# FFN output products of a hybrid layer as seven block products in one sweep over all tokens

## The chip, the cores and the metric

One core of a Trainium2 chip runs the whole layer as one program. The metric is the device time of one execution in microseconds (us), as the median of several runs. Beside the runs one execution was profiled; all rows below come from its trace.

## What is computed

The layer is one block of a decoder with 1024 tokens and a width of 1024. The parts that matter here are the two feed-forward networks (FFN), which have the same form:

```
def _swiglu(x, w_in, w_out):
    h = x @ w_in                                  # 1024x1024 @ 1024x5632
    gate, up = jnp.split(h, 2, axis=-1)           # 2816 columns each
    return (jax.nn.silu(gate) * up) @ w_out       # 1024x2816 @ 2816x1024

x = _layer_norm(ALPHA * x + 0.5 * _swiglu(x, ffn1_w_in, ffn1_w_out), ln1_g, ln1_b)
proj = x @ mix_w_in                               # z_a, z_u, z_v, two gates
...                                               # SSM branch, gMLP branch, merge, LN2
x = _layer_norm(ALPHA * x + 0.5 * _swiglu(x, ffn2_w_in, ffn2_w_out), ln3_g, ln3_b)
x = x + sigmoid(x @ ple_w_gate) * (p @ ple_w_proj)
```

All data is float32. Each operand of a product is cut into a high part and a low part (both float32r), and a product is the sum of three: high x high, high x low, low x high.

## The kernel before

**Engines.** TensorE executes in the order of the program text. ScalarE and VectorE get an order that a scheduler works out when the kernel is built, from its own estimate of times; a group at the start is an exception. Loads of weights go out on SP's queue, stores and loads of residual rows on POOL's. `split(hi, lo, src)` (L72) makes the parts of an operand: a ScalarE copy with a cast (L74) and a VectorE subtraction (L75).

**Jobs.** All weight loads of the kernel form one list (`add_job`, `make_jobs`, L204). Raw tiles of 128x1024 (512 KB) come through three buffers (`RAWBUFS`), split tiles `hi` and `lo` through five of each (`WBUFS`). `take(key, AHEAD)` asks for a job and for the three after it. Work that is to run between later matmuls is put off with `defer(us, key, fn)`: `tick()` in the product loops runs what is due by a running sum of TensorE time, and `need(key)` runs it at the latest.

**Gate and up products (`hidden`, L506).** There are 22 steps f. Each makes the gate and the up block of 128 columns for all tokens, as seven block products (Strassen in Winograd's form) of 12 matmuls of 128x128 by 128x512. The sums of weights for a step are made by `pair_steps` (L282) on VectorE. Of the three PSUM banks of a step, `b1` is copied out and added to further: the product that follows the next one waits for the copy. The results stay in `es` (tiles `e0` to `e3`; `e0` and `e1` have two buffers, the others one) and are stored to DRAM, `g_d[f]`, by two DMAs (L556). Two pairs of FFN 2 are split during FFN 1 (`PRE_AT`), stored, and loaded again.

**Output products (`out_phase`, L563).** Tokens are eight tiles (tt) of 128 rows, done in three sweeps (`SWEEPS`): tiles 0 to 2, 3 to 5, 6 and 7. A sweep holds two PSUM banks of 128x512 for each tile and goes over all 22 chunks f. For each f it needs the 128x1024 rows of `w_out`, split (kept for the last five f between sweeps, else loaded again), and the activations of its tiles, 128x384 or 128x256, loaded by `load_g` and split (L74 `gh`, L75 `gl`). The first two chunks are split before the phase begins (`early`, tile `ge`). At a sweep's end VectorE adds the banks to the residual row tile y (L609), then `norm_tile` (L436) normalizes y, TensorE transposes it and `to_T` splits it into `xh` and `xl` (L75), and POOL multiplies and adds the norm's vectors for the residual (`keep`, L736 and L737). In the sweeps that are followed by another, this is put off by 6 to 18 us of TensorE time.

**What follows.** After FFN 1 `z_block` (L757) multiplies the new x by the weights of z_v, z_a and z_u, four token tiles at a time with four split units on the chip. `snake` (L478) goes through the four units forward and backward in turn; the turn is kept over the whole kernel. After FFN 2 the last stage (`ppg`, `ppp`) uses the same `snake`, two token tiles at a time.

## Time and profile before

| | us |
|---|---|
| median of 3 runs | 2128.04 (2123.31 to 2128.73) |
| the profiled execution | 2132.67 |
| its span, first to last instruction | 2130.9 |
| gate and up products of FFN 1, one step of 22 | 19.6 |
| output phase of FFN 1 (first output matmul to first of z_v) | 471.2 to 723.5 |
| output phase of FFN 2 (to the end of its matmuls) | 1754.8 to 2006.2 |

The profiled execution is 4.6 us above the median of the runs, and its span is 1.8 us short of its time. Busy time of TensorE counts matmuls that overlap in its pipeline, so that a mean duration near 400 ns in a row says nothing of the pace; the distance between two starts does.

### The profile page before, as it was taken

The numbers are of one execution on the slowest core, as the hardware profiler recorded it, in microseconds if no ns is written. First come the engines' busy times: TensorE is split into PE (matmuls) and PEld (weight loads), VectorE is DVE, ScalarE is ACT, GpSimd is POOL, SyncE is SP. The second block draws the span as 40 slices with busy tenths as digits, with TensorE's granted clock in tenths as the row PEclk, the third lists the DMA queues.
The fourth block names the chain that finished last, engine by engine and source line by source line (L and its number), as shares of the span: only waits on it lengthen the run. The fifth ranks groups of instructions, "written<-read, shape, count | busy, mean of one in ns | idle before, by whom it ended". The sixth has DMA issues, their size and how long they took to land.

```text
span 2130.9 us, 25814 instructions
## 1 busy us (share of the span) xinstructions
PE 2104.5 (99%) x9471; PEld 1718.0 (81%) x9471; DVE 1264.3 (59%) x2327; ACT 796.5 (37%) x1317; POOL 314.0 (15%) x367
## 2 busy tenths in 40 slices
...
GB/s 139 89 79 159 89 142 105 79 142 251 120 222 139 195 56 50 74 82 71 99 55 233 288 229 238 96 82 80 89 69 80 89 100 313 149 165 141 151 60 40
DMA packets 212413, 273.21 MB, mean 128 GB/s; under 512 B 18196, under 2 KB 159088, under 8 KB 212288
## 3 DMA queue, kind: packets, MB, share of 16 engines
...
## 4 chain that ended last, share of the span: by engine, by line
PE 84%; issue 6%; DVE 5%; DMA 2%; ACT 1%; POOL 1%; SPq 0%; POOLq 0%; DVEq 0%; ACTq 0%
PE p_f L502 36%; PE po_f L465 8%; PE po_f L463 8%; PE po_f L464 8%; PE ppg L464 1%; PE ppg L463 1%; PE ppg L465 1%; PE po_mo L463 1%; PE po_mo L464 1%; PE po_mo L465 1%; PE pgb L463 1%; PE pga L463 1%; PE pga L464 1%; PE pga L465 1%; PE pgb L464 1%
## 5 line engine op out<-in xcount | busy, mean ns | idle before, releaser
L75 DVE TENSOR_TENSOR wl<-wr,wh 128x1024 fp32r<-128x1024 f32 (+1 forms) x212 | 253.0, 1196 | 129.6 <-ACT wh L74 129.6
L74 ACT CAST wh<-wr 128x1024 fp32r<-128x1024 f32 (+1 forms) x212 | 203.4, 960 | 223.8 <-issue 43.0
L463 PE MATMUL po_f<-wh,gh 128*128 128x512 f32 x680 | 270.8, 398 | 0.0
L465 PE MATMUL po_f<-wh,gl 128*128 128x512 f32 x680 | 268.8, 395 | 0.0
L464 PE MATMUL po_f<-wl,gh 128*128 128x512 f32 x680 | 268.7, 395 | 0.0
L556 POOL DMA_DIRECT2D g_d<-e_f x88 | 47.9, 544 | 776.3 <-DVE e_f L553 742.3
L74 ACT CAST gh<-gr_f 128x384 fp32r<-128x384 f32 (+1 forms) x128 | 60.9, 476 | 245.8 <-PE po_f L464 206.5
L465 PEld LDWEIGHTS po_f<-wh,gl 128*128 128x128 f32 x680 | 127.6, 188 | 31.1
L464 PEld LDWEIGHTS po_f<-wl,gh 128*128 128x128 f32 x680 | 127.7, 188 | 29.9
L463 PEld LDWEIGHTS po_f<-wh,gh 128*128 128x128 f32 x680 | 127.7, 188 | 29.8
L75 DVE TENSOR_TENSOR gl<-gr_f,gh 128x384 fp32r<-128x384 f32 (+1 forms) x128 | 67.0, 527 | 114.7 <-ACT gh L74 114.1
L292 DVE TENSOR_TENSOR s<-wr 128x512 f32<-128x512 f32 x44 | 30.9, 703 | 165.4 <-DMA wr<-in_ffn_w_in_dram 165.4
L75 DVE TENSOR_TENSOR wlt<-s,wht 128x1024 fp32r<-128x1024 f32 x44 | 53.9, 1226 | 53.4 <-ACT wht L74 51.0
L74 ACT CAST whs<-s 128x1024 fp32r<-128x1024 f32 x44 | 46.1, 1049 | 80.7 <-PE p_f L502 71.9
L74 ACT CAST wht<-s 128x1024 fp32r<-128x1024 f32 x44 | 46.1, 1048 | 76.4 <-PE p_f L502 76.0
L502 PE MATMUL p_f<-T3l,wht 128*128 128x512 f32 (+3 forms) x184 | 72.2, 393 | 1.9 <-DVE T3l L75 1.9
L502 PE MATMUL p_f<-B11l,wha 128*128 128x512 f32 (+3 forms) x184 | 72.1, 392 | 1.5 <-DVE B11l L75 1.5
L502 PE MATMUL p_f<-T4h,wh 128*128 128x512 f32 (+3 forms) x184 | 72.1, 392 | 0.8 <-ACT e_f L546 0.8
L75 DVE TENSOR_TENSOR xl<-xf_x,xh 128x512 fp32r<-128x512 f32 x32 | 62.8, 1969 | 16.9 <-ACT xh L74 16.8
L502 PE MATMUL p_f<-T4l,wh 128*128 128x512 f32 (+3 forms) x184 | 72.1, 392 | 0.4 <-DVE T4l L75 0.4
L502 PE MATMUL p_f<-T3h,wht 128*128 128x512 f32 (+3 forms) x184 | 72.3, 393 | 0.0
L502 PE MATMUL p_f<-B11h,wha 128*128 128x512 f32 (+3 forms) x184 | 72.2, 392 | 0.0
...
## 6 DMA issues: line engine op xcount, KB each, us to landing
wr<-in_ffn_w_out_dram SPq DMA_DIRECT2D x112, 512.0 KB, 3.7
wr<-in_ffn_w_in_dram SPq DMA_DIRECT2D x88, 512.0 KB, 4.2
...
wr<-in_mix_w_in_dram SPq DMA_DIRECT2D x28, 512.0 KB, 3.8
x_d<-y POOLq DMA_DIRECT2D x16, 512.0 KB, 4.3
...
xs<-in_x_dram SPq DMA_DIRECT2D x8, 512.0 KB, 8.3
```

The source lines that it names most:

```text
L74: ACT.copy(out=hi, in_=src)
L75: DVE.tensor_sub(out=lo, in0=src, in1=hi.bitcast(F32))
L292: DVE.tensor_tensor(out=s1, in0=a21, in1=a22, op=ALU.add)
L463: PE.matmul(acc, lhsT=ah, rhs=bh, start=start, stop=False)
L464: PE.matmul(acc, lhsT=ah, rhs=bl, start=False, stop=False)
L465: PE.matmul(acc, lhsT=al, rhs=bh, start=False, stop=stop)
L502: PE.matmul(acc[:, cs], lhsT=p, rhs=q, start=start and k == 0 and i == 0, stop=stop and k == HK - 1 and i == 2, skip_group_check=True)
L556: nc.gpsimd.dma_start(out=g_d[f][:, h * HT:(h + 1) * HT], in_=es[h])
```

## The change

Both output phases become seven block products in the same Winograd form as the gate and up products. The 2x2 blocks are: tokens in two halves of 512 (four tiles each), hidden columns in pairs of chunks (even and odd f), and output columns in two halves of 512. A product goes over 11 chunk pairs, and its four PSUM banks (one for each token tile of a half) stay open over the next products: each is evicted after a product and then added to. So each product evicts 128x512 four times, 28 times in all, and the token tiles 0 to 3 are complete after the fifth product and the tiles 4 to 7 after the seventh (`OUT`, `out_strassen`).

Operands that are sums are made before. After each odd step `hidden` makes four sums of activations on VectorE (`total`) and stores seven blocks of 128x512 in place of two for each of two steps. A job `wsum` for each pair of chunks loads two row tiles of `w_out`, makes four differences in place on VectorE and stores both tiles to DRAM (`wt_d`). In the output phase each of the 77 units then loads 128x512 of weights and 128x512 of activations by two DMAs into one raw tile, which is split as a whole.

The rest follows from the order: all eight residual tiles of FFN 1 have buffers of their own; `norm_half` puts off the first half's tiles in steps of 11 us and the second half's in steps of 6.5 us; the second half of z_v is done tile by tile (five calls of `snake` where there were two); units of the stage after the phase are no longer asked for inside it; and the pre-made pairs and the vector transposes move.

```diff
-SWEEPS = ((0, 1, 2), (3, 4, 5), (6, 7))
 PSWEEPS = ((0, 4, 1), (5, 2, 6), (3, 7))
-PRE_AT = (9, 15)
-LN_US = 13.0
+OUT = (("S1", "T1", False, 1, 1, True, False), ("S4", "B22", True, 0, 1, True, False),
+       ("A12", "B21", False, 0, 0, True, False), ("A11", "B11", False, 0, 0, False, False),
+       ("S2", "T2", True, 0, 1, False, True), ("S3", "T3", True, 1, 1, False, False), ("A22", "T4", True, 1, 0, True, True))
+GX = ("A11", "A12", "A22", "S1", "S2", "S3", "S4")
+NP = NF // 2
+PRE_AT = (8, 14)
 LN2_US = 13.0, 10.0, 8.5
...
+    def ffn_jobs(nm, w_in, w_out, g_d):
+        rows = lambda f: w_out[f * P:(f + 1) * P, :]
         for f in range(NF):
             pair = lambda w, f: [[(0, 1024, cols(w, f * P, P))], [(0, 1024, cols(w, FF + f * P, P))]]
             if nm == "f1" and f in PRE_AT:
                 add_job(("pre", PRE_AT.index(f)), "pre", pair(w2i, PRE_AT.index(f)))
+            if f % 2:
+                add_job((nm, "ws", f // 2), "wsum", [[(0, 1024, rows(f - 1))], [(0, 1024, rows(f))]])
             add_job((nm, "h", f), "pair", [] if nm == "f2" and f < len(PRE_AT) else pair(w_in, f))
-        out_jobs(nm, w_out, NF, sweeps)
-
+        for p, (a, b, *_) in enumerate(OUT):
+            for i in range(NP):
+                y, x = {"T1": (0, 0), "T3": (0, 1), "T4": (1, 0), "T2": (1, 1)}.get(b, (int(b[1]) - 1, int(b[2:] or 0) - 1))
+                w = wt_d[nm][i][y] if b[0] == "T" else rows(2 * i + y)
+                add_unit((nm, "s", p, i), [(0, 512, w[:, x * 512:(x + 1) * 512]), (512, 512, g_d[i][a])])
+    g1_d, g2_d = ([{x: dram.tile([P, HT], F32, name=f"g_{nm}_{i}_{x}") for x in GX} for i in range(NP)] for nm in ("f1", "f2"))
+    wt_d = {nm: [[dram.tile([P, D], F32, name=f"wt_{nm}_{i}_{y}") for y in range(2)] for i in range(NP)] for nm in ("f1", "f2")}
...
+            elif kind == "wsum":
+                (b11, b12), (b21, b22) = ((r[:, :512], r[:, 512:]) for r in loaded[li:li + 2])
+                for o, x, y in ((b11, b12, b11), (b12, b22, b12), (b22, b22, b11), (b21, b21, b22)):
+                    DVE.tensor_tensor(out=o, in0=x, in1=y, op=ALU.subtract)
+                for y in range(2):
+                    nc.gpsimd.dma_start(out=wt_d[key[0]][key[2]][y], in_=loaded[li + y])
...
-    def norm_tile(y, tt, nm, transposed, keep, wait=0.0, ln_us=LN_US):
-
-
-        def first():
-            normalize(y, D, f"{nm}_{tt}")
-            defer(ln_us + wait / 2, ("x", tt), lambda: transposed((0,)))
+    def norm_tile(y, tt, nm, transposed, keep, t0, t1, wait=0.0):
         def rest():
             transposed((1,))
             keep()
         if wait:
-            defer(wait, ("x", tt), first)
+            defer(wait, ("n", tt), lambda: normalize(y, D, f"{nm}_{tt}"))
         else:
-            first()
-        defer(wait * 1.5 + ln_us + 1.9 + (4.0 if wait else 0.0), ("x", tt), rest)
+            normalize(y, D, f"{nm}_{tt}")
+        defer(t0, ("x", tt), lambda: transposed((0,)))
+        defer(t1, ("x", tt), rest)
+    def norm_half(y, tt, *a):
+        h, j = divmod(tt, 4)
+        if h:
+            norm_tile(y, tt, *a, 9.0 + 6.5 * j, 11.5 + 6.5 * j)
+        else:
+            norm_tile(y, tt, *a, 17.0 + 11.0 * j, 21.0 + 11.0 * j, 3.0 + 11.0 * j)
...
             if cs.stop == HT:
-                for h in range(2):
-                    nc.gpsimd.dma_start(out=g_d[f][:, h * HT:(h + 1) * HT], in_=es[h])
+                def put(x, g):
+                    nc.gpsimd.dma_start(out=g_d[f // 2][x], in_=g)
+                def total(x, o, a, b, op):
+                    DVE.tensor_tensor(out=o, in0=a, in1=b, op=op)
+                    put(x, o)
+                put("A12" if f % 2 else "A11", es[0])
+                if f % 2 == 0:
+                    a11, a21 = es[:2]
+                else:
+                    put("A22", es[1])
+                    ss = [ep.tile([P, HT], F32, name=f"g{b}_{nm}_{f}", tag=f"e{b}", bufs=1) for b in (2, 3, 4)]
+                    total("S1", ss[0], a21, es[1], ALU.add)
+                    total("S2", ss[1], ss[0], a11, ALU.subtract)
+                    total("S3", a21, a11, a21, ALU.subtract)
+                    total("S4", ss[2], es[0], ss[1], ALU.subtract)
...
+    def out_strassen(nm, y_of, after, hook=None):
+        last = job_at[nm, "s", len(OUT) - 1, NP - 1]
+        ys, count = {}, 0
+        for p, (_, _, more, h, dh, fresh, end) in enumerate(OUT):
+            if not more:
+                acc = [bank(f"po_{nm}_{p}_{t}") for t in range(4)]
+            for g in ((0, 1),) + tuple((i,) for i in range(2, NP - 2)) + ((NP - 2, NP - 1),):
+                ops = [take((nm, "s", p, i), max(min(AHEAD, last - job_at[nm, "s", p, i]), 0)) for i in g]
+                for t in range(4):
+                    tick()
+                    for i, (hi, lo) in zip(g, ops):
+                        c = slice(512 + t * P, 512 + (t + 1) * P)
+                        for k, (a, b) in enumerate(((hi, hi), (hi, lo), (lo, hi))):
+                            PE.matmul(acc[t], lhsT=a[:, c], rhs=b[:, :512], start=not more and i == 0 and k == 0,
+                                      stop=i == NP - 1 and k == 2, skip_group_check=True)
+                        pe_us[0] += 3 * 0.233
+                    if g[-1] == NP - 1:
+                        tt, ds_ = 4 * h + t, slice(dh * 512, (dh + 1) * 512)
+                        y = ys[tt][:, ds_]
+                        if fresh:
+                            DVE.scalar_tensor_tensor(out=y, in0=y, scalar=ALPHA, in1=acc[t], op0=ALU.mult, op1=ALU.add)
+                        else:
+                            DVE.tensor_tensor(out=y, in0=y, in1=acc[t], op=ALU.add)
+                        if end:
+                            after(tt, ys[tt])
+                count += len(g)
+                if count % 2 and len(ys) < NT and count > 2:
+                    tt = (len(ys) + 4) % NT
+                    ys[tt] = y_of(tt)
+                if hook is not None:
+                    hook(count)
...
+    yp = y_stack.enter_context(pool("y1", NT, side="right"))
...
-    out_phase("f1", NF, y_load(yp, "1", lambda tt: x_v[tt]), after1,
-              lambda si, f: next(prm, None) if f >= 2 else None)
+    out_strassen("f1", y_load(yp, "1", lambda tt: x_v[tt]), after1, lambda n: next(prm, None) if n % 2 == 0 else None)
...
+    def z_block(nm, lhs, evac, by_tile=False):
         us = [unit((nm, q), 512) for q in range(4)]
         for half in range(2):
+            if half and by_tile:
+                for tt in range(4, 8):
+                    need(("x", tt))
+                    acc = bank(f"p{nm}_{tt}")
+                    snake([acc], KD, lambda i, k: (lhs(xh, k, tt), lhs(xl, k, tt)), lambda k: at(us[k // 2], slice(None), k % 2),
+                          lambda i, acc: evac(tt, acc))
+                break
...
+            z_block("zv", nat, ev_v, True)
...
-    out_phase("f2", NF, x2, after3)
+        norm_half(y, tt, "x3", lambda qs: to_T(y, xh, xl, tt, "x3", tmp, 3, qs), keep)
+    out_strassen("f2", x2, after3)
```

## Rows read from the trace of the kernel before

**Rows 1.** The page: busy time of each engine, and the chain of waits by engine.

```profile
PE 2104.5 (99%) x9471; PEld 1718.0 (81%) x9471; DVE 1264.3 (59%) x2327; ACT 796.5 (37%) x1317; POOL 314.0 (15%) x367
...
PE 84%; issue 6%; DVE 5%; DMA 2%; ACT 1%; POOL 1%; SPq 0%; POOLq 0%; DVEq 0%; ACTq 0%
```

**Rows 2.** Waits of TensorE, longest first: total us, times, longest.

```profile
PE ssm_y L1367 <- DVE ssm_h L1360: 2.9, 2, 1.5
PE po_mo L463 <- DVE sga L934: 2.9, 1, 2.9
```

**Rows 3.** Busy time of each engine in stretches, clock, DMA share, GB/s.

```profile
core 0: us, PE busy (x) PEld busy (x) DVE busy (x) ACT busy (x) POOL busy (x), PEclk, DMA share, GB/s
392.80:412.40 19.60, 19.60 (x85) 15.75 (x84) 10.22 (x14) 7.08 (x10) 1.08 (x2) 1.00 0.27 81
471.20:723.50 252.30, 252.30 (x1114) 203.50 (x1113) 167.68 (x333) 108.48 (x180) 47.65 (x34) 1.00 0.60 197
...
723.50:768.30 44.80, 44.80 (x202) 36.18 (x201) 36.77 (x85) 17.04 (x31) 19.09 (x11) 1.00 0.24 79
1754.80:2006.20 251.40, 251.40 (x1106) 203.07 (x1105) 171.53 (x238) 108.25 (x180) 42.56 (x26) 1.00 0.57 191
1757.00:1790.00 33.00, 33.00 (x144) 26.72 (x143) 22.28 (x25) 12.85 (x19) 5.65 (x11) 1.00 0.99 374
1944.50:2006.20 61.70, 61.70 (x280) 49.92 (x279) 50.94 (x72) 38.89 (x68) 17.39 (x6) 1.00 0.60 197
```

**Rows 4.** Timeline of TensorE, two stretches: start, us, instruction; 35 and 14 between.

```profile
471.20 0.39 PE L463 MATMUL po_f<-wh,ge 128*128 128x512 f32 x1
...
479.18 0.40 PE L465 MATMUL po_f<-wh,ge 128*128 128x512 f32 x1
...
2002.67 0.40 PE L463 MATMUL po_f<-wh,gh 128*128 128x512 f32 x1
...
2005.94 0.40 PE L465 MATMUL po_f<-wh,gl 128*128 128x512 f32 x1
```

**Rows 5.** Stretches, for instructions on tile po_f alone (FFN 1's phase).

```profile
471.00:760.00 289.00, 249.52 (x1056) 196.98 (x1056) 10.71 (x16) 1.00 0.55 181
```

**Rows 6.** The page: DMA issues, median us to landing.

```profile
wr<-in_ffn_w_out_dram SPq DMA_DIRECT2D x112, 512.0 KB, 3.7
```

**Rows 7.** Timelines of ScalarE and VectorE at the end of FFN 2's output phase.

```profile
2004.97 1.05 ACT L74 CAST wh<-wr 128x1024 fp32r<-128x1024 f32 x1 [3.14 <-PE po_f L465]
...
2008.92 1.18 DVE L75 TENSOR_TENSOR wl<-wr,wh 128x1024 fp32r<-128x1024 f32 x1
```

**Rows 8.** DMA issues between 1757 and 1800 us.

```profile
wr<-in_ffn_w_out_dram SPq DMA_DIRECT2D x9, 512.0 KB, 7.2
```

**Rows 9.** Timelines of VectorE and ScalarE in a step of `hidden` from 392.80.

```profile
393.00 0.69 DVE L552 SCALAR_TENSOR_TENSOR e_f<-e_f,p_f 128x512 f32<-128x512 f32 x1
...
398.57 0.69 DVE L292 TENSOR_TENSOR s<-wr 128x512 f32<-128x512 f32 x1 [4.28 <-DMA wr<-in_ffn_w_in_dram]
...
395.80 0.59 ACT L535 COPY e_f<-p_f 128x512 f32<-128x512 f32 x1 [2.37 <-PE p_f L502]
```

**Rows 10.** Groups of VectorE's instructions, 1944.5 to 2006.2 us: busy, mean ns.

```profile
L75 DVE TENSOR_TENSOR wl<-wr,wh 128x1024 fp32r<-128x1024 f32 x20 | 27.8, 1395 | 7.3 <-ACT wh L74 7.3
L75 DVE TENSOR_TENSOR xl<-xf_x,xh 128x512 fp32r<-128x512 f32 x6 | 10.7, 1787 | 0.8 <-ACT xh L74 0.8
L75 DVE TENSOR_TENSOR gl<-gr_f,gh 128x256 fp32r<-128x256 f32 x17 | 6.9, 421 | 2.5 <-ACT gh L74 2.4
L376 DVE TENSOR_SCALAR xa<-xa,mv_x,rs_x 128x1024 f32<-128x1024 f32 x3 | 2.4, 797 | 0.0
```

**Rows 11.** Timeline of VectorE in the last sweep of FFN 1.

```profile
682.30 0.69 DVE L75 TENSOR_TENSOR xl<-xf_x,xh 128x512 fp32r<-128x512 f32 x1 [0.83 <-ACT xh L74]
...
703.00 2.88 DVE L75 TENSOR_TENSOR xl<-xf_x,xh 128x512 fp32r<-128x512 f32 x1
```

**Rows 12.** Timeline of TensorE after its wait at 1212 us.

```profile
1215.03 0.68 PE L463 MATMUL po_mo<-wh,gh 128*128 128x512 f32 x1 [2.85 <-DVE sga L934]
...
1218.49 0.46 PE L465 MATMUL po_mo<-wh,gl 128*128 128x512 f32 x1
```

47 lines of the change are left out of this document (12 added, 35 removed).

## The prediction

> **What bounds the kernel now.** I read four views in this order. First the page's busy times and its chain of waits: TensorE is busy 99% of the span and carries 84% of the chain [rows 1]. That alone does not say that it never waits, so next come its waits: the longest single one is 2.9 us, and no entry of the list is longer in total [rows 2]. Then the stretches: in both FFN output phases and in one step of the gate and up products TensorE is busy all the time at full clock, with VectorE at 52 to 68% and DMA at 27 to 60% [rows 3]. In these stages time is therefore the number of matmuls times their spacing. The spacing is the last view: 15 output matmuls start 0.2336 us apart, (2005.94 - 2002.67) / 14 [rows 4]; I use 0.2333, which is also the 19.6 us of a step over its 84 matmuls [rows 3]. The reader should see that nothing but TensorE ends last here, and that VectorE, with 50.9 of the 61.7 us of the last sweep [rows 3], is the engine with least room.
>
> **What is removed.** One output phase now has 22 x 8 x 2 x 3 = 1056 matmuls, which the trace counts [rows 5]. The seven products have 7 x 11 x 4 x 3 = 924. The difference is 132 for each FFN, 264 in all, at 0.2333 us: **-61.6 us**. An output phase is 252.3 and 251.4 us now [rows 3], and would be about 221.
>
> Could the spacing itself change? The 36 matmuls on an activation tile that holds high and low part side by side start 0.228 us apart, (479.18 - 471.20) / 35 [rows 4]. The new units put both operands in one tile, which is another layout again. If the new matmuls went at that pace, 1848 x 0.0053 = 9.8 us more would go. I take 0, as 0.233 is what the steps and the sweeps show, and keep -10 for the range.
>
> **Feeding the products.** Each unit is 512 KB (weights 256, activations 256) and serves 12 matmuls, 2.8 us. In the first sweep today 704 KB serve 18 matmuls, 4.2 us. So the need is 187 GB/s against 172. A raw buffer is held for the landing (3.7 us for 512 KB [rows 6]), the cast on ScalarE (1.05) and the low part on VectorE (1.18, both [rows 7]), and an estimated 0.3 for signals: 6.2 us, over three buffers 2.1 us a unit. That is inside 2.8, so the cost is 0 and the cover is 0.7 us a unit. VectorE needs 1.2 + 4/11 x 0.69 = 1.5 us a unit, ScalarE 1.05.
>
> At the start of the sweep that cover is gone. Eight residual tiles of 512 KB and the norms' vectors load on POOL's queue. In FFN 2 today the same burst fills the DMA engines for 33 us [rows 3], and the weights land in 7.2 us [rows 8]. A unit then takes (7.2 + 2.5) / 3 = 3.2 us, and some ten units come 0.4 us late each, 4 us in a phase. At that point two units are made and three raw tiles are loaded, 14 us of work. I take **+1 us** for both phases; the ends are 0 and 8.
>
> **Sums during gate and up products.** For two steps of f VectorE gets four sums of activations and four of weights, 128x512 each, 0.69 us like the weight sum of today [rows 9]: 5.5 us in 39.2. A step goes from 10.2 [rows 3] to 13.0 us of VectorE in 19.6. DMA for two steps goes from 3 MB to 5.9 MB (six loads and two stores of 512 KB, seven stores of 256 KB): some 155 GB/s, where 374 have been moved [rows 3]. POOL issues nine DMAs in place of four. All of it hides behind 19.6 us of matmuls. What is queued behind the sums is the next step's first copy out of PSUM. Its target has two buffers, and one now stays in use until the third sum has read it. The step's last VectorE operation ends 0.9 us after the boundary (392.80, then 393.00 + 0.69), three sums bring this to 3.0, the copy (0.59) to 3.6 [rows 9]. TensorE needs that bank two products, 5.6 us, after the boundary: 2.0 us of cover. One more weight split ahead of the sums eats 1.2 of it. The three raw buffers also pass six tiles in two steps, not four; VectorE already waits 4.28 us for a raw tile in a step [rows 9] without TensorE waiting. I take **+2 us** over the 22 boundaries of both FFNs; the ends are 0 and 11 (0.5 each).
>
> **The last two products of each FFN.** Four tiles are normalized and transposed in these 61.6 us, where the last sweep has three. From the last sweep's VectorE time, 50.9, go 17 activation splits (6.9); to it come two weight splits (2.8), four evictions (2.8) and a fourth tile: two low parts 3.6, the scaling 0.8, and an estimated 2.5 for two statistics of 0.69 and ten small operations [rows 10]. That is 56.5 us of 62 to 65. It fits, but TensorE has only three units, 8.4 us, ready ahead. A tile is dear because a low part takes 0.69 us alone and 2.88 us while POOL multiplies the tile [rows 11]. I take **+3 us** for both FFNs; the ends are 0 and 10.
>
> This bears on a rule of the Trainium skill, SBUF — State Buffer, "Who interferes with whom": VectorE and GpSimd share a port by an exclusive lock, and the loser blocks fully. The trace agrees in kind. If POOL's 5.8 us for a tile (17.4 / 3) were lost to VectorE entirely, and not the 3.5 that the means contain (2 x 1.1 and 20 x 0.2 / 3), an estimate by that page adds 4 x 2.3 = 9 us, 65 us of VectorE work, and a wait of some 2 us for each FFN. The sum goes by the rows.
>
> **The second half's tiles.** Tiles 4 to 7 now end together; today only two do. After FFN 1 VectorE is busy 36.8 of 44.8 us in the z_v block [rows 3]; two more tiles add 2 x 6.9 = 13.8, so 50.6 of 49 (44.8 and the 4.2 us while the last product's banks finish). The norms of z_v can slip, the transposes cannot: tile 7 must be there 39.2 us on. Taking tiles one by one also makes five snaking calls of two: z_a starts with its fourth unit, whose buffer comes free only 1.4 us earlier, while cast and low part take 2.2. I take **+5 us**; the ends are 0 and 12.
>
> After FFN 2 the same odd count of calls turns the order of the last stage: it starts with its fourth unit, in a buffer that the last product frees 0.7 us before. Today a unit's low part starts 2.9 us after its cast ends there (2006.02 and 2008.92 [rows 7]), held by the norms of two tiles; now there are four. So -0.7 + 1.05 + 2.9 + 1.2 = 4.5 us after the boundary. Such a wait has a second price: after the 2.9 us wait matmuls start 0.43 us apart, at the lower of the two clock levels (1.2 GHz), (1218.49 - 1215.03) / 8 [rows 12], and eight at 0.2 lose 1.6. I take **+5 us**; the ends are 0 and 11.
>
> The moved pre-made pairs, the vectors turned earlier and the other deferral arguments change no work: 0.
>
> **Sum.** -61.6 + 1 + 2 + 3 + 5 + 5 = -45.6 us. The profiled execution took 2132.7 us with a span of 2130.9; it would take 2087. The median of the runs is 4.6 us lower, 2128.0, so I give **2082 us** for the runs.
>
> **Rivals.**
> (a) *Nearly all the gain comes.* The waits at the ends hide behind a better order on VectorE, as in the last sweep today, where TensorE is busy 61.7 of 61.7 us [rows 3]. Then the waits total under 8 us: 2066 to 2074, or down to 2060 with part of the shorter spacing. Against it: the two starts with a fourth unit.
> (b) *VectorE becomes the bound at the ends.* With POOL's stretches the last two products and the stages after them run at VectorE's pace. The upper ends add up, 10 + 12 + 11, with the sums' 11 and the burst's 8: 52 us, so 2118; a typical case, with half of the sums and the burst, gives 2108. For it: 56 of 62 us. Against it: nothing stalls at 51.
> (c) *The feed is the bound, and the kernel is slower.* The place is the raw buffers. Break-even is a unit of 3.2 us, 154 x 0.4 = 61.6: a buffer held 9.6 us, a landing of 7.1. In the burst landings are 7.2 [rows 8]. If they reach 7.5 all through the sweeps, units take 3.33 us, and 154 x 0.53 = 82 us are lost, 20 more than gained: about 2148. Against it: the FFN 1 phase moves 197 GB/s over 252 us [rows 3], and TensorE does not wait. A rule of the Trainium skill speaks for it (DMA: Bandwidth & Descriptors, "Bandwidth"): transfers should be 1 MiB or more, and smaller ones lose rate; here they shrink to 256 KB. The trace so far differs, as 374 GB/s have been moved by pieces of 192 and 512 KB in flight together.
> (d) *The sums move the waits into the gate and up stages*, 2 us at each of 22 boundaries, with the upper ends at one FFN's end: within 0.3% of before, some 2124.
>
> **Chances.** The forecast (waits of 8 to 28 us, 2074 to 2095) 0.52; (a) 0.22; (b) 0.16; (d) 0.04; (c) 0.06. From these, faster by over 0.3% (about 6 us, what a measurement can tell from no change) is 0.52 + 0.22 + 0.16 = 0.90, within it 0.04, slower 0.06. The range reaches from (a) with half the spacing gain to just short of the typical case of (b): 2060 to 2106, leaving out some 0.17.
>
> **What the profile after would show.** Right: 924 output matmuls a phase, 0.233 us apart, phases of 219 to 226 us; ScalarE waiting for TensorE to free buffers, not for loads, in the middle products; VectorE near 66% in the gate and up steps and near 90% in the last two products; short TensorE waits for low parts at the first z_a and the first last-stage matmuls. The forecast is wrong if TensorE waits in mid-sweep while ScalarE waits for loads (c), if every second step of f has a wait for the copy (d), or if no wait shows at the ends (a).

## The result, and the profile after

The changed kernel takes **2160.1 us** (median of 4 runs, 2158.2 to 2168.8) where the kernel before takes 2128.4 beside it: 1.0162 of the time, 95% interval 1.013 to 1.0194. It is slower, by some 32 us; 2082 was forecast, 46 less than before. The profiled execution took 2158.2 us with a span of 2156.1.

The page of the changed kernel, busy times and chain:

```profile
PE 2047.6 (95%) x9207; PEld 1680.9 (78%) x9207; DVE 1355.0 (63%) x2437; ACT 785.5 (36%) x1227; POOL 363.2 (17%) x477
...
PE 39%; issue 36%; DVE 9%; DMA 7%; POOL 5%; ACT 2%; SPq 1%; POOLq 0%; DVEq 0%; ACTq 0%
```

The 264 matmuls are gone (9471 in [rows 1], 9207 here), but TensorE, which was busy 99% of the time and carried 84% of the chain [rows 1], now carries 39% of it. Its waits, total us, times, longest:

```profile
PE p_f L517 <- ACT e_f L550: 19.0, 19, 4.1
PE ppg L479 <- DVE wl L81: 11.7, 1, 11.7
PE p_f L517 <- ACT e_f L554: 10.9, 14, 1.2
PE po_f L659 <- ACT wh L80: 10.0, 2, 8.8
PE pzv L480 <- DVE xl L81: 7.3, 3, 3.9
PE xt_x_T L723 <- DVE B11l L81: 6.5, 2, 6.3
PE po_f L659 <- DVE y L666: 5.7, 1, 5.7
```

Before, no single wait was longer than 2.9 us, and no entry of the list was larger in total [rows 2]. Where the time went shows when the span is cut at the first matmul of each stage. The view of stretches of the changed kernel (columns as in [rows 3]): gate and up products and output phase of FFN 1, z_v, z_a, then FFN 2's two stages and the last stage:

```profile
25.10:501.90 476.80, 450.13 (x2012) 365.96 (x2011) 317.30 (x524) 177.75 (x259) 72.65 (x122) 0.98 0.49 162
501.90:723.70 221.80, 216.06 (x965) 178.58 (x964) 150.76 (x273) 94.26 (x116) 36.33 (x32) 0.98 0.65 216
723.70:786.20 62.50, 52.02 (x225) 41.65 (x225) 57.11 (x144) 26.68 (x53) 30.70 (x18) 0.92 0.21 76
786.20:857.50 71.30, 67.34 (x292) 62.86 (x291) 32.38 (x73) 15.50 (x27) 14.44 (x20) 0.97 0.23 67
1328.50:1788.30 459.80, 446.23 (x1949) 363.25 (x1949) 274.36 (x397) 165.15 (x247) 50.26 (x93) 0.98 0.44 149
1788.30:2020.00 231.70, 218.82 (x958) 178.79 (x956) 155.75 (x177) 94.71 (x116) 31.90 (x26) 0.97 0.63 207
2020.00:2156.00 136.00, 119.66 (x528) 96.24 (x528) 58.41 (x104) 35.67 (x67) 19.66 (x8) 0.95 0.15 54
```

The same cuts in both traces (the output phases of before are in [rows 3]; z_a is cut where the long run of z_u's products begins, so it holds the first of these), in us:

| stage | before | after | difference |
|---|---|---|---|
| start to the first gate product | 18.0 | 25.1 | +7.1 |
| gate and up products, FFN 1 | 453.2 | 476.8 | +23.7 |
| output products, FFN 1 | 252.3 | 221.8 | -30.5 |
| z_v | 46.5 | 62.5 | +16.0 |
| z_a | 65.8 | 71.3 | +5.5 |
| rest of the mixer, its output | 473.1 | 471.0 | -2.1 |
| gate and up products, FFN 2 | 445.9 | 459.8 | +13.8 |
| output products, FFN 2 | 251.4 | 231.6 | -19.7 |
| last stage | 124.7 | 136.1 | +11.4 |

The differences add up to 25.2 us, as the two spans differ; the medians differ by 32, as the profiled execution of before was some 4 us above its median and this one 2 below. The output phases give 50.2 us, near the forecast; the stages around them take 75 back. In them TensorE is no longer busy all the time (450 of 477 us, 52 of 62.5) and the granted clock is below 1.00.

**A boundary of two steps in the gate and up products.** The step after f = 17 begins at 420.2 us. Timeline of VectorE, then of ScalarE, then of TensorE, changed kernel:

```profile
406.16 1.42 DVE L243 TENSOR_TENSOR wr<-wr,wr 128x512 f32<-128x512 f32 x2 [3.88 <-DMA wr<-in_ffn_w_out_dram]
...
416.80 1.23 DVE L81 TENSOR_TENSOR wla<-wr,wha 128x1024 fp32r<-128x1024 f32 x1 [4.35 <-ACT wha L80]
...
424.01 0.68 DVE L567 SCALAR_TENSOR_TENSOR e_f<-e_f,p_f 128x512 f32<-128x512 f32 x1
...
425.94 0.68 DVE L574 TENSOR_TENSOR e_f<-e_f,e_f 128x512 f32<-128x512 f32 x1
...
415.72 1.05 ACT L80 CAST wha<-wr 128x1024 fp32r<-128x1024 f32 x1 [2.60 <-DMA wr<-in_ffn_w_in_dram]
...
426.69 0.59 ACT L550 COPY e_f<-p_f 128x512 f32<-128x512 f32 x1 [3.99 <-PE p_f L517]
...
425.47 0.40 PE L517 MATMUL p_f<-T1h,wls 128*128 128x512 f32 x1
427.33 0.50 PE L517 MATMUL p_f<-T2h,whs 128*128 128x512 f32 x1 [1.47 <-ACT e_f L550]
```

Read it as one chain. VectorE stands 3.88 us at the weight difference (L243) until its raw tile has landed; the pair's tiles follow late through the same buffers, so ScalarE's cast waits for a load and VectorE's low part 4.35 us for the cast. The step's last gate operation (L567) therefore starts 3.8 us after the boundary, where it was 0.2 [rows 9]; the third sum (425.94) ends at 426.6, and the copy that needs its buffer starts at 426.69. TensorE's third product begins at 427.3 instead of 425.7, one spacing behind the matmul before it.

### The profile page after: what moved, and what is told of

It is laid out like the page before. It is cut to its first block, busy times and chain, and to the rows that moved or that the text cites. A ratio compares the mean times of both kernels' runs of the same rounds, so it can differ in the third digit from the quotient of the medians.

```text
span 2156.1 us, 25757 instructions
## 1 busy us (share of the span) xinstructions
PE 2047.6 (95%) x9207; PEld 1680.9 (78%) x9207; DVE 1355.0 (63%) x2437; ACT 785.5 (36%) x1227; POOL 363.2 (17%) x477
## 4 chain that ended last, share of the span: by engine, by line
PE 39%; issue 36%; DVE 9%; DMA 7%; POOL 5%; ACT 2%; SPq 1%; POOLq 0%; DVEq 0%; ACTq 0%
PE po_f L659 14%; PE p_f L517 2%; DVE wl L81 2%; POOL g_f_S L571 2%; DMA wr<-g_f_S 2%; DMA wr<-in_ffn_w_out_dram 1%; PE ppg L479 1%; POOL g_f_A L571 1%; PE ppg L480 1%; PE ppg L478 1%; DMA wr<-in_ffn_w_in_dram 1%; PE pgb L478 1%; PE pgb L479 1%; PE pgb L480 1%; PE pga L478 1%
## 5 line engine op out<-in xcount | busy, mean ns | idle before, releaser
L659 PE MATMUL po_f<-wh 128*128 128x512 f32 x616 | 243.9, 396 | 15.7 <-ACT wh L80 10.0
L659 PE MATMUL po_f<-wl,wh 128*128 128x512 f32 x616 | 242.4, 394 | 2.4 <-DVE wl L81 2.4
L659 PE MATMUL po_f<-wh,wl 128*128 128x512 f32 x616 | 241.7, 392 | 0.0
L659 PEld LDWEIGHTS po_f<-wh 128*128 128x128 f32 x616 | 116.9, 190 | 41.0 <-ACT wh L80 17.0
L659 PEld LDWEIGHTS po_f<-wl,wh 128*128 128x128 f32 x616 | 117.1, 190 | 27.6 <-DVE wl L81 3.8
L659 PEld LDWEIGHTS po_f<-wh,wl 128*128 128x128 f32 x616 | 117.1, 190 | 24.6
L517 PE MATMUL p_f<-T2h,whs 128*128 128x512 f32 (+3 forms) x184 | 74.5, 405 | 19.2 <-ACT e_f L550 19.0
L517 PE MATMUL p_f<-T3h,wht 128*128 128x512 f32 (+3 forms) x184 | 73.4, 399 | 10.9 <-ACT e_f L554 10.9
L243 DVE TENSOR_TENSOR wr<-wr,wr 128x512 f32<-128x512 f32 x44 | 31.3, 712 | 74.1 <-DMA wr<-in_ffn_w_out_dram 73.5
L517 PE MATMUL p_f<-T2l,whs 128*128 128x512 f32 (+3 forms) x184 | 72.3, 393 | 0.5 <-DVE T2l L81 0.5
L550 ACT COPY e_f<-p_f 128x512 f32<-128x512 f32 (+3 forms) x46 | 26.1, 568 | 128.0 <-PE p_f L517 75.8
L517 PE MATMUL p_f<-B11h,wla 128*128 128x512 f32 (+3 forms) x184 | 72.4, 394 | 0.0
L517 PE MATMUL p_f<-T2h,wls 128*128 128x512 f32 (+3 forms) x184 | 72.4, 393 | 0.0
```

What stands on the lines that cost most here:

```text
L243: DVE.tensor_tensor(out=o, in0=x, in1=y, op=ALU.subtract)
L517: PE.matmul(acc[:, cs], lhsT=p, rhs=q, start=start and k == 0 and i == 0, stop=stop and k == HK - 1 and i == 2, skip_group_check=True)
L550: ACT.copy(out=s1, in_=b1[:, cs])
L659: PE.matmul(acc[t], lhsT=a[:, c], rhs=b[:, :512], start=not more and i == 0 and k == 0, stop=i == NP - 1 and k == 2, skip_group_check=True)
```

## The experiments

Each is an edit of the changed kernel unless it says otherwise. Times are medians; ratios are to the kernel before, run beside them.

**1. no_wdiff, no_gsum, ws_late: what makes the gate and up stages longer?**

```diff
 no_wdiff
-            if f % 2:
+            if False:
                 add_job((nm, "ws", f // 2), "wsum", [[(0, 1024, rows(f - 1))], [(0, 1024, rows(f))]])
...
-                w = wt_d[nm][i][y] if b[0] == "T" else rows(2 * i + y)
+                w = rows(2 * i + y)
 no_gsum
-                    ss = [ep.tile([P, HT], F32, name=f"g{b}_{nm}_{f}", tag=f"e{b}", bufs=1) for b in (2, 3, 4)]
-                    total("S1", ss[0], a21, es[1], ALU.add)
-                    total("S2", ss[1], ss[0], a11, ALU.subtract)
-                    total("S3", a21, a11, a21, ALU.subtract)
-                    total("S4", ss[2], es[0], ss[1], ALU.subtract)
+                    for x, b in (("S1", 1), ("S2", 0), ("S3", 1), ("S4", 0)):
+                        put(x, es[b])
 ws_late
-            if f % 2:
-                add_job((nm, "ws", f // 2), "wsum", [[(0, 1024, rows(f - 1))], [(0, 1024, rows(f))]])
             add_job((nm, "h", f), "pair", [] if nm == "f2" and f < len(PRE_AT) else pair(w_in, f))
+            if f % 2:
+                add_job((nm, "ws", f // 2), "wsum", [[(0, 1024, rows(f - 1))], [(0, 1024, rows(f))]])
```

> This kernel leaves the weight differences out: no loads of the output weight for them during the gate and up products, no subtractions, no stores; the products T1 to T4 read plain blocks of the weight instead, so the output is not the reference's. Theory R (the gate and up stages lose time because three raw buffers must pass six tiles in two chunks instead of four, which makes the pair splits late): the gate and up stage of FFN 1 goes from 476.8 us back to 431 to 453 and that of FFN 2 from 459.8 to 425 to 446, and the start to the first product from 25.1 back to about 18; with -7 at the start, -24 to -46 and -14 to -35 the kernel takes 2070 to 2115 us. Rival E (the loss comes from the two e0 and e1 buffers that the activation sums hold): the steps keep alternating between 19.3 and 20 to 25 us, only the start's 7 us and a few us more go, and the kernel takes 2140 to 2152 us.

> This kernel leaves the four activation sums S1 to S4 out (the four VectorE additions and their three tiles); tiles that are at hand are stored under their names, so the output is not the reference's, while every transfer and product stays. Theory R (raw buffers and late pair splits): the gate and up stages stay within 8 us of 476.8 and 459.8, the kernel at 2145 to 2158 us. Rival E (the sums hold e0 and e1, so the copy of the first product waits): the waits of the first product of a step on that copy go, the gate and up stages lose 20 and 12 us or more, and the kernel takes 2110 to 2128 us.

> Only the order of two jobs changes: the weight differences of a pair of chunks are queued behind the odd chunk's pair instead of ahead of it, so a pair's two raw loads come first and the four subtractions come later in VectorE's order; pair 0's no longer stand ahead of the first low parts. If the head of VectorE's line was what the start waited for, the first product begins at about 18 us instead of 25.1 and two of the three stretches at the low clock behind it go: -7 to -10. For the gate and up stages theory R says that the pair's tiles get their buffers earlier but the buffers still pass six tiles per two chunks, so half or less of the 24 and 14 us come back (-5 to -20); rival E says 0 there. Together 2128 to 2146 us by R, about 2149 by E.

Measured, with raw4f1 and ws_nosub (next) for comparison; start and stages in us:

| kernel | time | ratio | start | gate/up 1 | gate/up 2 |
|---|---|---|---|---|---|
| before | 2128.4 | | 18.0 | 453.2 | 445.9 |
| changed | 2160.1 | 1.0162 (1.013 to 1.0194) | 25.1 | 476.8 | 459.8 |
| no_wdiff | 2106.5 | 0.9885 (0.9864 to 0.9907) | 17.8 | 452.1 | 442.7 |
| no_gsum | 2166.9 | 1.0175 (1.0158 to 1.0192) | 25.6 | 485.6 | 457.7 |
| ws_late | 2129.0 | 0.9996 (0.9982 to 1.0011) | 17.9 | 469.3 | 446.7 |
| raw4f1 | 2149.6 | 1.0113 (1.009 to 1.0135) | 25.3 | 462.5 | 460.9 |
| ws_nosub | 2127.3 | 0.9988 (0.9978 to 0.9998) | 18.1 | 472.1 | 445.7 |

Without the weight differences these stages are back at the times of before; without the activation sums nothing is gained: rival E falls. (no_gsum comes out above theory R's range too, but its ratio is not clear of the changed kernel's.) Yet its symptom was in the trace, the copy L550 starting right behind the third sum. Why does its removal not help? Without the sums the wait moves to another copy. Waits of TensorE in no_gsum, and ScalarE's timeline at one of them:

```profile
PE p_f L517 <- ACT e_f L561: 30.9, 18, 4.7
```

```profile
428.17 1.04 ACT L80 CAST wha<-wr 128x1024 fp32r<-128x1024 f32 x1 [4.20 <-DMA wr<-in_ffn_w_in_dram]
429.12 0.58 ACT L561 COPY e_f<-p_f 128x512 f32<-128x512 f32 x1
```

The copy stands behind a cast that waits 4.20 us for its load. Both chains begin at a late load; which operation behind it TensorE comes to wait for changes from kernel to kernel. ws_late only changes the order of two jobs and is worth 31 us, as much as theory R gave it at the most. By stage it does not fit R: of FFN 2's 14 us 13 come back, where R gave half or less, and of FFN 1's 24 only 7.5.

At the start it is the head of the line alone. VectorE, then TensorE, changed kernel:

```profile
13.93 0.69 DVE L243 TENSOR_TENSOR wr<-wr 128x512 f32<-128x512 f32 x1 [4.79 <-DMA wr<-in_ffn_w_out_dram]
14.54 0.68 DVE L81 TENSOR_TENSOR B11l<-xt_x_B,B11h 128x512 fp32r<-128x512 f32 x1
...
15.28 1.11 PE L723 MATMUL xt_x_T<-ident,xd 128*128 128x128 f32 x4 [6.31 <-DVE B11l L81]
```

The first low part (B11l) stands behind a weight difference that nobody needs for some 480 us; ws_late and no_wdiff both give the 7 us back.

**2. raw4f1 and ws_nosub: the buffers, or VectorE standing at the load?**

```diff
 raw4f1
-        phase["pre"] = None, hs.enter_context(pool("pre"))
+        phase["pre"] = phase["pair"]
+        phase["more"] = hs.enter_context(pool("wmore"))
+        hs.callback(phase.pop, "more")
...
-            raw = wraw_p.tile([P, 1024], F32, name=f"wr{i}", tag="raw")
+            own = "more" in phase and jobs[ji][1] == "wsum" and i == first_load[ji]
+            raw = (phase["more"] if own else wraw_p).tile([P, 1024], F32, name=f"wr{i}", tag="raw")
 ws_nosub
-                for o, x, y in ((b11, b12, b11), (b12, b22, b12), (b22, b22, b11), (b21, b21, b22)):
-                    DVE.tensor_tensor(out=o, in0=x, in1=y, op=ALU.subtract)
```

> In FFN 1's gate and up stage alone, one of the two raw tiles of each pair's weight differences comes from a buffer of its own; the room is that of the small tiles of the two pre-made pairs, which now share the pair's. FFN 2's stage is as it was. Theory R (buffers): FFN 1's stage goes from 476.8 us to 455 to 465 while FFN 2's stays at 457 to 461, the kernel at 2138 to 2150 us. Rival D (not the buffers but the place of the four subtractions in VectorE's order): FFN 1's stage stays within 5 us of 476.8, the kernel at 2153 to 2163 us.

> The changed kernel without the four subtractions of each pair's weight differences; the two raw loads, their buffers and the two stores stay, so the output is not the reference's. It parts what no_wdiff took away together. If the pair's raw loads are late because the buffers must pass two more tiles, FFN 1's stage stays within 8 us of 476.8 and FFN 2's within 6 of 459.8, and only the start's 7 us go: 2145 to 2156 us. If it is VectorE, which stands at the first subtraction until its load has landed with everything else behind it, the stages go to about 452 and 443 as in no_wdiff, and the kernel to 2105 to 2118 us.

A further buffer takes 14 of FFN 1's 24 us and leaves FFN 2's stage, which did not get it, alone: buffers matter. But without the subtractions, with every load and buffer kept, FFN 2's stage is cured (445.7) and most of FFN 1's ordinary steps too: they take 19.3 to 19.6 us. The time, 2127.3 us, lies between the ranges of the two answers. What is left in FFN 1, 472.1, lies mainly at the two pre-made pairs (steps of 27.1 and 28.5 us). There the queue of the loads itself stands at its buffers, held until a low part is made or a weight difference is stored. Waits of the load queue in ws_nosub, 180 to 216 us:

```profile
SPq L198 <- DVE wl L81: 21.6, 2, 12.2
SPq L198 <- DMA wt_f<-wr: 6.8, 2, 4.6
```

So both answers were half right, and not by place alone. raw4f1 cures ordinary steps as well: steps of 21.2, 21.7 and 21.5 us in the changed kernel take 19.3 there, though VectorE still does the subtractions. In an ordinary step the loss needs both, a load that the buffers let in late and an operation of VectorE that stands at it, and either remedy ends most of it. At the pre-made pairs the subtractions are not needed for it, and the further buffer takes only a part (the two steps at each pair take 42.7 and 44.6 us in raw4f1, 46.9 and 45.1 in the changed kernel, 39.3 and 39.7 in no_wdiff). How that rest divides between buffers and transfers was not tried.

**3. parity and parity2: the direction of the sweeps.**

```diff
                           lambda i, acc: evac(tt, acc))
+                snaked[0] = True   (parity);   snaked[0] = False   (parity2)
                 break
```

> Only the direction of the k sweeps after the tile-by-tile half of z_v is restored, so that z_a and the last stage's first block begin with the first weight unit instead of the fourth. Theory H (the hand-off's waits are for the fourth unit's low part, made too late for a reversed sweep): the waits of 3.72 us ahead of z_a and 11.66 us ahead of the last stage go with the low clock behind each (about 3 and 7 us), so -12 to -25 and 2133 to 2146 us. Rival N (VectorE is late with the last tiles' norms and splits anyway): the stage waits for a tile's low part instead and no more than 5 us is gained, 2153 us or more.

> The edit named parity set the flag to the value that it had, and left the order of the products as it was. Here the flag is cleared, so that z_a and the last stage's first block begin with the first weight unit. Theory H: the waits of 3.72 us ahead of z_a and of 11.66 us ahead of the last stage go, and with them the low clock behind each (10.3 and 13.6 us at half speed, so 5 and 7 us): up to -27, 2133 to 2148 us. Rival N (VectorE is late with the last tiles anyway, and the stage waits for a tile's low part instead): at most -5, 2153 us or more.

parity, which changed no product's order, took 2163.2 us and serves as a second run of the changed kernel. parity2 takes 2144.7 (1.0106, 1.0072 to 1.0139), in theory H's range. What the wait was, in the changed kernel (ScalarE, VectorE, TensorE):

```profile
2018.87 1.05 ACT L80 CAST wh<-wr 128x1024 fp32r<-128x1024 f32 x1 [2.25 <-PE po_f L659]
...
2020.70 1.27 DVE L666 SCALAR_TENSOR_TENSOR xa<-xa,po_f 128x512 f32<-128x512 f32 x2
...
2030.86 1.21 DVE L81 TENSOR_TENSOR wl<-wr,wh 128x1024 fp32r<-128x1024 f32 x1
...
2032.13 0.79 PE L479 MATMUL ppg<-wl,xh 128*128 128x512 f32 x1 [11.66 <-DVE wl L81]
```

The fourth unit's cast is done at 2019.9, its low part starts 10.9 us later, behind the evictions and norms of four tiles, and TensorE, which wants just this unit first, waits 11.66 us. With the first unit first it meets that low part long after. The price of the low clock was counted too high in what was expected: of the 13.6 us at a granted clock of 0.50 (2022.7 to 2036.3) TensorE spends 9.4 waiting anyway, and only the products of the other 4.2 are slowed. z_a and the last stage in parity2:

```profile
787.70:853.70 66.00, 65.76 (x293) 62.29 (x292) 32.70 (x73) 15.55 (x27) 14.41 (x20) 0.99 0.24 72
2014.70:2141.80 127.10, 119.33 (x529) 95.84 (x528) 62.22 (x104) 36.38 (x68) 19.97 (x8) 0.98 0.16 58
```

**4. load_sp: the burst of residual loads.**

```diff
-            nc.gpsimd.dma_start(out=y, in_=src(tt))
+            q.dma_start(out=y, in_=src(tt))
...
-    out_strassen("f1", y_load(yp, "1", lambda tt: x_v[tt]), after1, ...
+    out_strassen("f1", y_load(yp, "1", lambda tt: x_v[tt], nc.sync), after1, ...
...
-        nc.gpsimd.dma_start(out=y, in_=x2_d[tt])
+        nc.sync.dma_start(out=y, in_=x2_d[tt])
```

> The eight loads of the residual's tiles in each output phase are issued from SyncE's queue, between the weight units' loads, rather than from GpSimd's, where all eight go out within some 10 us of the phase's start. Theory B (the burst delays the units' loads): the waits of 8.80, 0.46, 0.65, 1.31 and 1.20 us at the start of FFN 2's output phase go with the low clock behind them (13.7 us at half speed), and the one of 5.75 us in FFN 1's with its 6.9 us of low clock: the phases go from 221.8 and 231.6 us to about 213 each, the kernel to 2130 to 2142 us. Rival V (the eviction after the first product is late by VectorE's order, and the units wait for their buffers): FFN 1's phase stays at 218 to 222, FFN 2's loses at most 10, the kernel is at 2148 us or more.

It takes 2149.3 us (1.011, 1.0081 to 1.0139), and the phases go to 219.6 and 225.8: rival V's numbers, not theory B's. The burst in the changed kernel, queue by queue at FFN 2's start:

```profile
1796.90 2.10 POOL L1030 DMA_DIRECT2D xa<-x_d  x4 [2.36 <-DMA g_f_S<-g_f]
...
1804.93 0.53 POOL L1030 DMA_DIRECT2D xa<-x_d  x1 [1.17 <-DMA lnb<-in_ln_b_dram]
...
1798.19 1.49 SPq L198 DMA_DIRECT2D wr<-g_f_S  x1
...
1818.00 1.04 ACT L80 CAST wh<-wr 128x1024 fp32r<-128x1024 f32 x1 [20.17 <-DMA wr<-g_f_S]
...
1819.10 0.80 PE L659 MATMUL po_f<-wh 128*128 128x512 f32 x1 [8.80 <-ACT wh L80]
```

Eight tiles, 4 MB, are issued within 8.6 us; a unit whose second load goes out beside them at 1798 is cast 20 us later, and TensorE runs out of the units that it has. In load_sp this wait is gone, but another of 6.8 us for an eviction (of xa, whose tile is loaded later now) stands in its place. So B's mechanism was there, but its gain was not: the burst delays the units, and the first tiles must not come late (in best two are issued earlier).

**5. no_keep: GpSimd's passes beside VectorE's.**

```diff
-            POOL.tensor_tensor(out=y, in0=y, in1=gb[0], op=ALU.mult)
-            POOL.tensor_tensor(out=y, in0=y, in1=gb[1], op=ALU.add)
...
-            POOL.tensor_tensor(out=y, in0=y, in1=gb3[0], op=ALU.mult)
-            POOL.tensor_tensor(out=y, in0=y, in1=gb3[1], op=ALU.add)
```

> GpSimd's two passes over each normalized tile after FFN 1 and after FFN 2 (the residual's scale and shift) are left out, so the output is not the reference's. Theory P (VectorE's passes take up to four times as long beside a pass of GpSimd: 2.43 us rather than 0.21 for a 128x1 one): z_v goes from 62.5 us to 48 to 55, the last stage loses 2 to 6 of its 136.1, the kernel is at 2140 to 2150 us. Rival S (the order of the norms and of the due times, not the slow passes): z_v stays above 58 us, the kernel at 2153 us or more.

2141.9 us (1.0081, 1.0051 to 1.0111), with z_v at 47.3 us where before has 46.5: the passes are nearly all of z_v's loss. VectorE and GpSimd in the changed kernel's z_v:

```profile
756.62 0.21 DVE L383 SCALAR_TENSOR_TENSOR rs_v<-rs_v 128x1 f32<-128x1 f32 x1
...
758.01 2.43 DVE L383 SCALAR_TENSOR_TENSOR rs_v<-rs_v 128x1 f32<-128x1 f32 x1
...
758.04 2.38 POOL L795 TENSOR_TENSOR y<-y,lng 128x1024 f32<-128x1024 f32 x1
```

An operation on one number a partition takes 0.21 us, and 2.43 when it meets a pass of GpSimd; it ends with it (760.44 and 760.42). So the small operations of a norm, which I had at 2.5 us together with its two statistics, can cost that much one by one when GpSimd is at work. The Trainium skill, SBUF — State Buffer, "Who interferes with whom", says that the loser of the shared port blocks for the other's whole instruction; these rows agree, with ends 0.02 us apart. The starts (758.01 and 758.04) do not tell who was first.

**6. best, best_r4, best2: do the parts add up?** best takes ws_late, parity2 and load_sp together, with these lines besides; best_r4 adds raw4f1's; best2 puts the loop of `keeps` under `with tc.issue_after(last["p"].ins)`.

```diff
-PRE_AT = (8, 14)
+PRE_AT = (9, 15)
...
+        def more_y():
+            tt = (len(ys) + 4) % NT
+            ys[tt] = y_of(tt)
+
+        more_y()
+        more_y()
         for p, (_, _, more, h, dh, fresh, end) in enumerate(OUT):
...
-                if count % 2 and len(ys) < NT and count > 2:
-                    tt = (len(ys) + 4) % NT
-                    ys[tt] = y_of(tt)
+                if count in (2, 4, 8, 11, 14, 16):
+                    more_y()
...
-        norm_half(y, tt, "x1", lambda qs: to_T(y, xh, xl, tt, "x1", tmp, 1, qs), keep)
+        norm_half(y, tt, "x1", ..., keep if tt < 4 else lambda: keeps.append(keep))
...
             z_block("zv", nat, ev_v, True)
+        for fn in keeps:
+            fn()
```

> The changed kernel with what the runs so far point to, and with the whole computation: weight differences behind the odd chunk's pair (ws_late measured -31 us), the pre-made pairs ahead of chunks 9 and 15 rather than 8 and 14 (in ws_late the longest waits left, 3.69 and 3.23 us, stand at them: -4 to -10), the sweep direction restored (parity2: -15), GpSimd's two passes over tiles 4 to 7 after FFN 1 put off until z_v is done (no_keep: -15 in z_v), residual loads from SyncE's queue with two of them ahead of the first product (load_sp: -11; two more waits of 6.8 and 3.0 us were left there: -11 to -18). If the losses are separate, as the theory has it, the sum is 2160 - 31 - 7 - 15 - 15 - 14 = 2078 us, 2068 to 2095, under both kernels. Rival: the losses hide one another (a stage freed of one wait meets the next, VectorE above all), and half or less of the parts adds up: 2105 us or more.

> As best, and in FFN 1's gate and up stage the further raw buffer of raw4f1. If buffers still hold the pairs back after the change of order, FFN 1's stage loses another 5 to 8 us against best's, and FFN 2's is the same; if the order was all, FFN 1's stage is within 3 us of best's.

> In best the passes of GpSimd over tiles 4 to 7 stayed where they were: they are later in the program's text, but GpSimd's queue was put in order by when they are ready, and z_v took 62.4 us again. Here they are queued behind the last of z_v's own GpSimd passes, with the whole computation done. Theory P: z_v goes to 47 to 51 us, and the kernel from 2089 to 2074 to 2080 us. Rival: the passes slow VectorE just as much in z_a, whose weights it splits then, or the state-space work behind them on GpSimd comes late by their 20 us: 2084 us or more.

best takes 2089.4 us (0.9817, 0.9794 to 0.9839), best_r4 2101.7 (0.9872, 0.9854 to 0.989), best2 2090.8 (0.9816, 0.9802 to 0.9829). All parts of best but one add up (2160 - 31 - 7 - 15 - 14 = 2093); GpSimd's passes did not move, and z_v stayed at 62.4. In best2 they did: z_v 49.2, but z_a 74.5, as TensorE waits 7.0 us for the copy of za, which itself stands behind the late passes (ScalarE's wait names GpSimd's L802), as the late tiles still hold its memory; the rest went in FFN 1's output phase (5 us more than in best). The loss was moved, not removed: the rival's range, by a way that it did not name.

best_r4 is the surprise: the buffer that gave 14 us in raw4f1 costs 11 here (FFN 1's stage 475.2 against best's 464.0). ScalarE's timeline in best_r4 shows where TensorE's waits come from:

```profile
177.95 0.59 ACT L553 COPY e_f<-p_f 128x512 f32<-128x512 f32 x1 [6.05 <-DMA g_f_S<-g_f]
...
179.38 0.59 ACT L555 COPY e_f<-p_f 128x512 f32<-128x512 f32 x1
```

The target of the first copy is a single buffer that holds a sum until its store has landed, and TensorE waits 15.6 us in all for the second (L555), which comes behind it. A form of rival E's mechanism thus exists; it was only not what bound the changed kernel. The wait itself is not new: between 18 and 475 us the same copy waits 26.6 us in best, in 9 times of at most 3.8, and TensorE waits once, 3.3 us, for the copy behind it; in best_r4 it is 34.8 us in 7 times of at most 6.7. Why it is longer there was not followed up.

**7. The pads: a pace that no step foresaw.** In the changed kernel products of one shape follow one another faster than before, so that the waits add more than the table of stages shows. It is plainest in the up projection, whose 384 products the change does not touch. Stretches of that stage alone in five kernels, in the order before, changed, pad_before, pad_after, pad64_after:

```profile
1118.50:1208.10 89.60, 89.60 (x386) 71.97 (x385) 41.38 (x57) 10.86 (x15) 13.55 (x25) 1.00 0.76 256
```

```profile
1138.30:1226.20 87.90, 87.90 (x385) 72.12 (x384) 41.45 (x57) 10.88 (x15) 13.51 (x25) 1.00 0.79 264
```

```profile
1103.53:1190.60 87.07, 87.07 (x386) 72.07 (x385) 41.38 (x57) 10.90 (x15) 13.50 (x25) 1.00 0.78 264
```

```profile
1141.76:1231.35 89.59, 89.59 (x385) 71.96 (x384) 41.58 (x58) 10.86 (x15) 13.51 (x25) 1.00 0.79 260
```

```profile
1138.61:1225.67 87.06, 87.06 (x385) 72.07 (x384) 41.47 (x57) 10.87 (x15) 13.51 (x25) 1.00 0.77 256
```

TensorE is busy throughout, the clock is 1.00, the work the same; 384 products take 89.6 or 87.1 us, 0.2333 or 0.2267 each. The edit, in the kernel before as in the changed one (16 for the 64 bytes):

```diff
     vecs = const.tile([P, P], F32, name="vecs")
+    pad = const.tile([P, 8], F32, name="pad")
+    POOL.memset(pad, 0.0)
```

> The changed kernel with one more tile of 32 bytes a partition among the constants, so that the weight tiles and everything behind them lie 32 bytes further on. In the profile of the changed kernel the products of 512 columns follow one another every 0.2305 us in the gate and up stages, 0.2271 in the output products, 0.2276 to 0.2290 in most of the mixer, where the kernel before has 0.2333 in all of them, at the granted clock of 1.00; the constants lost a tile of 520 bytes to another pool. Theory A (the pace hangs on where the operands lie): all of these go back to 0.2333, which over 3864, 1848 and some 1500 products is 11 + 11 + 8 = 30 us, and the kernel takes 2180 to 2195 us. Rival (the pace has another cause, as the transfers or the order): the pace stays, and the kernel within 4 us of 2160.

> As pad_after, with 64 bytes instead of 32. If what counts is the place within 64 bytes, pace and time are those of the changed kernel, 2160 us within 4; if it is a coarser one, the pace differs again.

> The kernel before with one more tile of 32 bytes among its constants and nothing else. Theory A: the gate and up stages, the output products and the mixer take up the faster pace, and the kernel goes from 2128 to 2090 to 2102 us without any change of its work. Rival: 2124 to 2132 us.

> The kernel before with a tile of 64 bytes among its constants. If the place within 64 bytes counts, nothing changes: 2124 to 2132 us, and a spacing of 0.2333.

| mean spacing, us | gate/up | output products | gates | up | last stage | time |
|---|---|---|---|---|---|---|
| before | 0.2333 | 0.2331 | 0.2332 | 0.2333 | 0.2332 | 2128.4 |
| pad_before | 0.2280 | 0.2280 | 0.2333 | 0.2267 | 0.2272 | 2093.4 |
| pad64_before | 0.2333 | 0.2331 | 0.2340 | 0.2334 | 0.2332 | 2127.7 |
| changed | 0.2305 | 0.2271 | 0.2280 | 0.2289 | 0.2333 | 2160.1 |
| pad_after | 0.2334 | 0.2271 | 0.2334 | 0.2334 | 0.2332 | 2166.5 |
| pad64_after | 0.2284 | 0.2271 | 0.2333 | 0.2267 | 0.2278 | 2161.3 |

(Mean distance of neighbouring 512-column products of a stage in the timeline, those under 0.3 us.) Theory A holds, and most plainly in pad_before: 32 unused bytes make the kernel before 1.6% faster (0.984, 0.982 to 0.986), 64 do nothing (0.9994, 0.9983 to 1.0005). In the changed kernel the same shift costs only 6 us of the 20 to 35 that I expected: the output products keep their 0.2271 with both pads, and stages that wait for loads take nothing from a quicker TensorE (FFN 1's gate and up stage takes 476.8 us at 0.2305 and 476.7 at 0.2334 in pad_after). With the pads the coarser place shows too: the gates and the last stage swap their paces between the changed kernel and pad64_after.

**8. best_pad and best3.** best_pad is best with the 64 bytes; best3 gives the two passes over tiles 4 to 7 to VectorE besides.

```diff
-            POOL.tensor_tensor(out=y, in0=y, in1=gb[0], op=ALU.mult)
-            POOL.tensor_tensor(out=y, in0=y, in1=gb[1], op=ALU.add)
+            eng = POOL if tt < 4 else DVE
+            eng.tensor_tensor(out=y, in0=y, in1=gb[0], op=ALU.mult)
+            eng.tensor_tensor(out=y, in0=y, in1=gb[1], op=ALU.add)
...
+        with tc.issue_after(last["v"].ins):
+            for fn in keeps:
+                fn()
```

> best with 64 bytes more among the constants. In pad64_after the gate and up stages' spacing went from 0.2305 to 0.2284 us and the last stage's from 0.2333 to 0.2278, while the gates' went from 0.2280 to 0.2333: over 3864, 384 and some 770 products -8 - 2 + 4 = -6 us. Where best is free of the waits that swallowed this in pad64_after (2161.3 against 2160.1), it shows: 2080 to 2086 us, under the 2093 of pad_before. If the stages wait for transfers and VectorE as much as they gain, 2086 to 2092.

> best_pad, and the two passes over tiles 4 to 7 after FFN 1 are VectorE's, queued behind the last of its own passes of z_v, instead of GpSimd's (8 passes of 1.2 us rather than 2.5, and none beside them). Theory P: z_v goes from 62.4 us to 47 to 51 as in no_keep and best2, and z_a keeps best's 66 since the stores that its buffer waits for go out earlier: 12 to 15 us under best_pad. Rival: z_a waits for its weights' low parts behind the passes, as it waited in best2: within 5 us of best_pad.

best_pad takes 2087.5 us (0.981, 0.9791 to 0.983), in the second case's range: no gain that is clear of best's noise (0.9817, 0.9794 to 0.9839). best3 takes **2077.3** (0.9763, 0.9741 to 0.9784), some 10 under best_pad: theory P, a little short. FFN 1's output phase, z_v, z_a, FFN 2's output phase and the last stage in best3:

```profile
477.90:700.00 222.10, 217.41 (x966) 179.08 (x965) 151.41 (x273) 94.03 (x116) 31.82 (x24) 0.98 0.63 217
700.00:752.50 52.50, 49.28 (x225) 40.21 (x224) 43.99 (x145) 26.72 (x53) 8.87 (x6) 0.97 0.16 51
752.50:818.00 65.50, 65.26 (x292) 62.03 (x292) 41.28 (x82) 15.01 (x27) 17.60 (x24) 1.00 0.33 105
1732.80:1953.70 220.90, 217.04 (x957) 178.20 (x956) 155.03 (x177) 94.43 (x116) 27.81 (x18) 0.98 0.64 217
1953.70:2078.90 125.20, 117.22 (x529) 95.91 (x528) 60.20 (x104) 36.33 (x68) 20.56 (x8) 0.98 0.17 59
```

This beats the kernel before by 2.4%, but against pad_before, which has the same pace, it is 16 us of 2093, not 51. Against pad_before the output phases give 50 us and the gate and up stages take back 27 (459.6 against 444.7, 447.2 against 434.9).

## Why the prediction was wrong

- **What bounds the kernel before**: right, and with a gap. TensorE's matmuls times their spacing is the time, but 0.2333 us was taken for a constant. It belongs to this kernel's layout (pad_before: 0.2280).
- **What is removed**: right. The phases have 924 products each, and were expected near 221 us; they took 221.8 and 231.6, and 222.1 and 220.9 in best3. A spacing of 0.2271 came on top, which I had kept as an end of the range only: 1848 x 0.0062 = 11 us. At that spacing the products alone take 420 of the 453 us; the rest is waits, the low clock behind them, and transposes. That the changed kernel's first phase met 221 is thus partly luck: the quicker pace made up for waits that I had put near nothing.
- **Feeding the products**: right in mid-sweep (from 560 to 700 us ScalarE's casts wait 66.2 us for TensorE to free buffers and 2.4 for loads, so rival (c)'s lack of feed does not occur), mis-sized at the start: the burst was put at 1 us for both phases, where TensorE waits 8.8 us for one unit, and load_sp is worth 11 (8 of them in the two phases).
- **Sums during gate and up products**: this is the step that failed, +2 us against 37.5, and nearer 48 when the quicker pace is counted (44 steps of 84 products, 3696 x 0.0028 = 10). It priced what is added by the busy time of VectorE, 13.0 us in 19.6, and found room. The room is there (VectorE is busy 317 of 477 us). What it did not price is where an engine that works in order stands while its operand is on its way: "VectorE already waits 4.28 us for a raw tile in a step [rows 9] without TensorE waiting" was taken as cover, when it was slack already spent. The six tiles through three buffers were named in the same sentence, and given no price. The cover of 2.0 us that was worked out for the copy was sound arithmetic on the wrong cause: no_gsum takes the sums away and nothing is gained. Rival (d) named the symptom, waits at the copy, and blamed the same innocent sums.
- **A place that no term covers**: the start. The first weight difference was put ahead of the first low parts in VectorE's order: +7.1 us, shown by ws_late.
- **The last two products, the second half's tiles**: the mechanisms were right, the terms mis-sized. +13 us was expected of these two items, and z_v, z_a and the last stage lost 32.9. In the last two products themselves, put at +3, hardly anything was lost (TensorE is busy 61.70 of 61.70 us from 662 and 60.54 of 61.00 from 1959). The reversed sweeps cost 14 (parity2: 5.3 in z_a, 9 in the last stage): the low part was put 2.9 us behind its cast, as two tiles' norms held it before, and was 10.9 behind it with four. GpSimd's passes cost 15 in z_v (no_keep): I had added VectorE's large operations at the mean of rows of before, and the chains of small operations as if they met no pass.
- **The rivals**: that the change ends slower had 0.06, for the feed of the output products. The loss came by rival (b)'s place, the ends, at about the upper ends that (b) adds up (10 + 12 + 11), and by (d)'s, the gate and up stages, at about its price (2 us at 22 boundaries is 44, 37.5 came). The sign given for (d), a wait for the copy in every second step, is what the trace shows, though from another cause. No rival had both at that size, and none had the start.
